# The second norm's second half is queued earlier, and three gate forms start 32 bytes further on

## The chip, the core and the metric

The kernel runs on one core of a Trainium2 chip. It is one program with five engines that run side by side and wait for each other through semaphores: PE (TensorE, matmuls; its weight loads have a row of their own, PEld), DVE (VectorE), ACT (ScalarE), POOL (GpSimd) and SP, which only issues DMAs. The metric is the device time of one execution in microseconds (us). Smaller is better.

## The reference, cut to what matters

One decoder layer for 512 tokens of width 1024, in float32. Two token mixers are merged; what this change touches comes behind them:

```python
x = x + rms_norm(mixed @ w_out, norm_mix_post)                      # first norm
h = rms_norm(x, norm_ffn_pre)                                       # second norm
f = (silu(h @ w_ffn_gate) * (h @ w_ffn_up)) @ w_ffn_down            # 1024 -> 2816 -> 1024
x = x + rms_norm(f, norm_ffn_post)
```

`rms_norm(x, g)` is `x * rsqrt(mean(x*x) + eps) * g`, with the mean over the 1024 channels of a token.

## The kernel before, in words

**Layout.** Channels lie on the 128 partitions, tokens along the free axis. So `x1[k]`, k = 0 to 7, is 128 channels by 512 tokens, and a mean over channels is a sum over partitions and over k. `halves[e]` are tokens 0 to 255 (e = 0) and 256 to 511 (e = 1). A float32 product is done as three matmuls in a rounded format: every operand is split into a high part and a low part (the rest), and high by high, high by low and low by high are added up in PSUM. Making such a pair ("a form") costs a copy on ACT for the high part and a subtraction on DVE for the low part, or two ACT steps and a DMA from POOL's queue that adds the raw matrix onto its negated high part (`dma_split`, L1523).

**The residual and the second norm.** `resid(e)` (L1413) multiplies the first norm's scale in, adds x and makes the high and low parts `h2h`, `h2l` (per k: DVE L1424, L1425, ACT L1426, DVE L1427). `resid_squares(e)` (L1431) squares `x1[k]` on ACT (L1436) and adds the eight squares up on POOL (L1439). `norm2_sums(e)` (L1443) sums them over the partitions with PE matmuls against ones (L251), makes mean + eps on DVE (L259) and takes the power -0.5 on POOL (L260). `norm2_scale(e, after)` (L1448) spreads the result over the partitions with PE (L268), and ACT copies it into `rb_x` (L1450).

**The channel mixer's first product.** `w_gate` and `w_up` have 22 column blocks of 128. The first three (`NPLAIN`) are plain products that need no scale beforehand, since the scale can be multiplied in afterwards. They cover the time in which the norm is made: `ffn_half(e, w, ps, ks)` (L1452) does, per row k, six matmuls of 256 tokens for gate and up of a block. Its weights are w0 and w1; the third block's, w2, run through `prod` with 512 tokens a matmul. From block N0 = 3 on, gate and up together are a 2 x 2 block matrix that is multiplied by the normalised `h` with seven half-size products in place of eight (a11, s2, s3, s1, a12, a22, s4; the scheme of Strassen and Winograd). A block of this kind is a unit (`unit(n)`, L1647), a product in it is twelve matmuls (L1662), and DVE adds its results together (L1668), which also frees the PSUM bank for the next. The units need the sums of the activations as forms of their own (b11, t2, t3, t1, b21, t4, b22), made once: `normed(e)` (L1606) multiplies the scale in, eight DVE steps a half (L1608); `x_form` (L1611) splits (high L1616, low L1617); `x_forms()` (L1627) makes the rest behind the second half's normalisation. Each unit also needs forms of its weights: `prep_g` (L1533) for the gate, `prep_u` (L1539) for a part of up, `prep_st` (L1574) for the four sums.

**Places.** Gate forms lie in turn in `wbuf` and in `g3`. `wbuf` holds two pairs of 1024 + 1024 columns; a pair starts `SHIFT` = 16 columns (64 bytes) further on, and for block N0+3 `TURN` = 8 columns (32 bytes) beyond that. `uub` has two halves, handed out in turn by `uu_half()` (L1340).

**What sets the order.** Each engine has one queue in an order fixed when the program is built, by dependences, by priorities and by the edges that the code adds: inside `tc.issue_after(x)` an instruction is queued behind x on x's engine. `tc.high_priority()` (used for the mean and the power) puts its instructions ahead where the data allow. `queued[...]` keeps instructions to queue others behind.

The calls around the change: `resid(1)` (L1767), rows 5 to 7 of w0's first half, `resid_squares(1)` (L1769), w1's first half with `norm2_sums(0)` in its middle, w0's second half with `norm2_scale(0)` behind its row 1, `normed(0)` and the form b11 (L1782 and L1783), w1's second half with `norm2_sums(1)` behind row 5 (L1784 to L1786), the first wide product of w2 with `norm2_scale(1)` behind its third row, form b21, `normed(1)`, and `x_forms()`.

Of the kernel before, what the change touches and what calls it, by code (L numbers as in the profile page):

```python
# [11 lines left out]
AF = mybir.ActivationFunctionType  # L12
OP = mybir.AluOpType
# [5 lines left out]
KD = D // 128  # L19
# [14 lines left out]
SHIFT = 16  # L34
TURN = 8
# [98 lines left out]
def hybrid_block_kernel(ctx: ExitStack, tc: tile.TileContext, I, outT):  # L134
    nc = tc.nc
    act, dve, pool, pe = nc.scalar, nc.vector, nc.gpsimd, nc.tensor
# [29 lines left out]
    g_fpre, g_fpost = vecs[:, 16:24], vecs[:, 24:32]  # L166
# [5 lines left out]
    rb_x = base.tile([128, S], F32, name="rb_x")  # L172
# [25 lines left out]
    for key in with_gla + with_cmp + with_att + late:  # L198
        kind, n = key
# [19 lines left out]
    def prod(ps, w, xh, xl, k0, kn, ktot, t=ALL):  # L219

        wh, wl = w
        marks = []
        for kk in range(kn):
            k = k0 + kk
            c = slice(kk * 128, (kk + 1) * 128)
            pe.matmul(ps[:, t], wh[:, c], xh(k)[:, t], start=(k == 0), stop=False)  # L226
            pe.matmul(ps[:, t], wh[:, c], xl(k)[:, t], start=False, stop=False)  # L227
            marks.append(pe.matmul(ps[:, t], wl[:, c], xh(k)[:, t], start=False, stop=(k == ktot - 1)))  # L228
        return marks
# [32 lines left out]
    broadcast, queued = [], {}  # L262
# [13 lines left out]
    for k in range(KD):  # L276
# [3 lines left out]
        if k == 0:  # L280
            act.activation(out=warm, in_=mhalf[:, 0:1], func=AF.Exp)
        last = act.activation(out=hT[:, k, :], in_=X[:, k], func=AF.Copy, scale=g_pre[:, k:k + 1])
        dve.scalar_tensor_tensor(out=hTl[:, k, :], in0=X[:, k], scalar=g_pre[:, k:k + 1],
                                 in1=hT[:, k, :].bitcast(F32), op0=OP.mult, op1=OP.subtract)
# [48 lines left out]
    halves = (slice(0, S // 2), slice(S // 2, S))  # L333
# [205 lines left out]
    for c in range(4):  # L539
        w = tk.next(("tok", 0, c))  # L540
# [78 lines left out]
    for j in range(NP):  # L619
# [6 lines left out]
        after = queued["dve"]  # L626
# [713 lines left out]
    def uu_half():  # L1340
        uturn[0] += 1
        return uub[:, 0:1024] if uturn[0] % 2 else uub[:, 1024:2048]
# [6 lines left out]
    def w_slot(which, shift=SHIFT):  # L1349

        if which == "w":
            return regions.next(shift)
        if which == "c":
            t = hlc(F32R, "w_hl")
            return [t[:, c:c + 1024] for c in (SHIFT, 1024 + SHIFT)]
        if which == "u":
            return uu_half(), uu_half()
        if which in ("d0", "d1"):
            t = wpair(which)
            return t[:, 0:1024], t[:, 1024:2048]  # L1360
        return tuple(wtile(t) for t in {"g3": ("g3h", "g3l"), "rw": ("rw", "rw")}[which])
# [6 lines left out]
    h2h, h2l = quads("h2h", 4, F32R, "hh"), quads("h2l", 2, F32R, "hl")  # L1368
    h2l23 = hlc(F32R, "h2l23")[:, 0:2048].rearrange("p (b a t) -> p b a t", b=2, a=2)
    h2l += [h2l23[:, i] for i in range(2)]  # L1370
    x1 = [slot(k) for k in range(8)]
# [41 lines left out]
    def resid(e, after=None, ks=range(KD), mult_after=None):  # L1413

        t = halves[e]
        if e not in rb_of:
            rb_of[e] = over_partitions(rs1, "tp", blocks[e], after)
        rb = rb_of[e]
        for k in ks:
            i, j = k // 2, k % 2  # L1420
            y = x1[k][:, t]
            hi, lo = h2h[i][:, j, t], h2l[i][:, j, t]
            with tc.issue_after(mult_after.ins) if mult_after else nullcontext():
                dve.tensor_tensor(out=y, in0=y, in1=rb[:, t], op=OP.mult)  # L1424
            dve.tensor_tensor(out=y, in0=y, in1=xs[i][:, j, t], op=OP.add)  # L1425
            last = act.activation(out=hi, in_=y, func=AF.Copy, scale=g_fpre[:, k:k + 1])  # L1426
            end = dve.scalar_tensor_tensor(out=lo, in0=y, scalar=g_fpre[:, k:k + 1], in1=hi.bitcast(F32),  # L1427
                                           op0=OP.mult, op1=OP.subtract)
        return last, end

    def resid_squares(e, ks=range(KD), after=None, squared_after=None):  # L1431
        t = halves[e]
        for k in ks:
            sq = sq2[0][:, t] if k == 0 else sq2[1 + (k - 1) % 6 // 2][:, halves[(k - 1) % 2]]
            with tc.issue_after(squared_after.ins) if squared_after else nullcontext():
                act.activation(out=sq, in_=x1[k][:, t], func=AF.Square)  # L1436
            if k > 0:
                with tc.issue_after(after.ins) if after else nullcontext():
                    pool.tensor_tensor(out=sq2[0][:, t], in0=sq2[0][:, t], in1=sq, op=OP.add)  # L1439

    rs2 = ffn.tile([128, NT], F32, name="rs2")

    def norm2_sums(e):  # L1443
        r = slice(2 * e, 2 * e + 2)
        ps = token_sums([sq2[0]], "tp", blocks[e])
        return rsqrt_mean(rs2[:, r], ps[:, r], D, EPS)

    def norm2_scale(e, after):  # L1448
        ps = over_partitions(rs2, "tp", blocks[e], after)
        return act.copy(rb_x[:, halves[e]], ps[:, halves[e]])  # L1450

    def ffn_half(e, w, ps, ks=range(KD)):  # L1452

        t = halves[e]
        marks = []
        for k in ks:
            i, j = k // 2, k % 2
            c = slice(k * 128, (k + 1) * 128)
            for x in range(2):
                wh, wl = w[x]  # L1460
                o = ps[x][:, t]
                pe.matmul(o, wh[:, c], h2h[i][:, j, t], start=(k == 0), stop=False)
                pe.matmul(o, wh[:, c], h2l[i][:, j, t], start=False, stop=False)
                last = pe.matmul(o, wl[:, c], h2h[i][:, j, t], start=False, stop=(k == KD - 1))
            marks.append(last)
        return marks
# [34 lines left out]
    N0 = NPLAIN  # L1501
# [29 lines left out]
        return minus  # L1531

    def prep_g(n, after=None):  # L1533
        hi, lo = w_slot(("w", "g3", "w")[(n - N0) % 3], SHIFT + (TURN if n == N0 + 3 else 0))
        minus = dma_split(n, hi, lo, raws[n, "w_gate"], I["w_gate"][n], after)
        forms[n, "a11"], forms[n, "a12"] = [(hi[:, c], lo[:, c]) for c in (slice(0, 512), slice(512, 1024))]
        return minus

    def prep_u(n, after=None, t=None):  # L1539
        t = uu_half() if t is None else t  # L1540
        hi, lo = t[:, 0:512], t[:, 512:1024]
        dma_split(n, hi, lo, ups[n][:, 512:1024], I["w_up"][n, :, 512:1024], after)
        forms[n, "a22"] = (hi, lo)
# [59 lines left out]

    XF = {}

    def normed(e):  # L1606
        for k in range(KD):
            dve.scalar_tensor_tensor(out=nb[k // 4][e][:, k % 4, :], in0=x1[k][:, halves[e]], scalar=g_fpre[:, k:k + 1],  # L1608
                                     in1=rb_x[:, halves[e]], op0=OP.mult, op1=OP.mult)

    def x_form(name, segs, after=None):  # L1611

# [144 lines left out]
    for n in (6, 7):  # L1757
        out_half(n, 1)
    sq2 = [t[:, i, :] for t in quads("sq2_", 2, F32, "e") for i in range(2)]
# [4 lines left out]
    on_act, on_dve = resid(0, None, range(KD - 1, KD), queued["mean"])  # L1764
    resid_squares(0, range(3, KD), root)
    marks = ffn_half(0, w0, first, range(3, 5))
    high_end, _ = resid(1, marks[-1])  # L1767
    ffn_half(0, w0, first, range(5, 8))
    resid_squares(1, range(KD), None, high_end)  # L1769
    split_pair(N0, s12, ("s1", "s2"), on_act, True)  # L1770
    w1 = (st.next(("g", 1)), st.next(("u", 1)))
    second = (bank("mm"), bank("mm"))
# [3 lines left out]
    marks = ffn_half(1, w0, first, range(0, 2))  # L1776
# [2 lines left out]
    nb = [[ffn.tile([128, 4, 256], F32, tag="a%d" % (2 * p + e), name="nb%d%d" % (p, e)) for e in range(2)]  # L1779
          for p in range(2)]  # L1780
    b11, b12, b21, b22 = [t.rearrange("p q t -> p (q t)") for t in (nb[0][0], nb[0][1], nb[1][0], nb[1][1])]
    normed(0)  # L1782
    x_form("b11", [(b11, *at(0))])  # L1783
    ffn_half(1, w1, second, range(0, 6))  # L1784
    scale_made = norm2_sums(1)
    ffn_half(1, w1, second, range(6, 8))  # L1786
    third = (bank("acc"), bank("acc"))

    def h2(p):
        return lambda k: p[k // 2][:, k % 2, :]  # L1790

    w2 = st.next(("g", 2))
    marks = prod(third[0], w2, h2(h2h), h2(h2l), 0, 3, KD)
    rb_made = norm2_scale(1, marks[-1])
    x_form("b21", [(b21, flat(quad("e0", F32R, "x4h")), flat(quad("e1", F32R, "x4l")))])
    normed(1)
    prod(third[0], [x[:, 384:1024] for x in w2], h2(h2h), h2(h2l), 3, 5, KD)
# [19 lines left out]
    for n in range(N0, KF):  # L1817
        if n + 2 < KF:
            load(n + 2, "w_gate")
            load(n + 2, "w_up")  # L1820
        last = unit(n, rest_of_forms if n == N0 else None,
                    (lambda copied: prep_u(N0 + 2, copied, uu_next)) if n == N0 + 2 else None)
        if n == N0:
            end = last
        if n == N0 + 1:
            plain_end()
            plain_out(2, *third)()
        if n + 1 < KF:
            prep_st(n + 1, end, plain_outs if n == N0 else None)
        if n + 2 < KF:  # L1830
            prep_g(n + 2, {N0 + 1: queued.get("s1cast"), N0 + 2: queued.get(("s34", N0 + 2)),
                           N0 + 3: queued.get(("s12", N0 + 4))}.get(n))
            if n == N0 + 1:
                uu_next = uu_half()
            if n > N0:
                prep_u(n + 2, queued["s1cast"] if n == N0 + 1 else None)
        if 2 * KH <= n < 2 * KH + 4:
            down_t3(n - 2 * KH)
# [352 lines left out]
```

## Time and profile before

| | us |
|---|---|
| median of 3 runs | 823.38 (822.57 to 823.55) |
| the profiled execution | 822.37 |
| its span, first to last instruction | 820.6 |
| PE busy | 813.5 |
| DVE busy | 649.5 |
| ACT busy | 523.6 |
| POOL busy | 177.4 |

The granted clock of TensorE was 1.00 of full speed (2.4 GHz) in the stretches around the change. A row of the order of time reads: start (us from the span's start), busy time, engine, line, operation, what it writes `<-` what it reads, the shape, the number of instructions merged into the row, and in brackets the idle time before it with what ended it. The busy time of one matmul row includes its way through the array, so the step from one start to the next, not the busy time, says how fast matmuls follow each other. A row of the waits reads: who `<-` for whom, total us, times, longest. A row of the stretches reads: window, its length, then busy time and number of instructions for PE, PEld, DVE, ACT and POOL, then the granted clock, the DMA engines' share and GB/s. Tiles go by the program's names without their numbers: `w_d`, `w_hl`, `w_g3h`, `w_rw`, `uub` and `wbuf` hold forms of weights, `hT_hi`, `hT_lo`, `x4h`, `x5h` and `x` forms of activations, `ps_...` are PSUM banks, `nb` the normalised activations, `sq` squares, `rs` the mean and its power.

### The profile page before, as it was taken

The page shows a single profiled execution, that of the slowest core. Times are in us where ns is not written, and L with a number is a line of the kernel's source. Part 1 is how long each engine was busy: PE and PEld are TensorE (multiplying, and loading weights), DVE is VectorE, ACT ScalarE, POOL GpSimd, SP SyncE. Part 2 cuts the span into 40 slices and gives each one's busy share as a digit, 9 for nine tenths or more (in the row PEclk, how much of TensorE's full clock was granted, in tenths as well). Part 3 has the DMA queues.
Part 4 walks back from the last instruction along what each step waited for, and adds up shares of the span by engine and source line. Part 5 has one row for each costly group of instructions (what it writes and reads, how often), then busy time and mean ns, then how long its engine had stood idle before and what let it go on. Part 6 is the DMA issues. An engine that isn't in the chain of part 4 may idle for free.

```text
span 820.6 us, 14977 instructions
## 1 busy us (share of the span) xinstructions
PE 813.5 (99%) x5676; PEld 750.2 (91%) x5676; DVE 649.5 (79%) x1219; ACT 523.6 (64%) x954; POOL 177.4 (22%) x221
## 2 busy tenths in 40 slices
PE   9999999999999999999999999999999999999997
PEld 8999999988888888888888999999999999889996
DVE  7878889955678988877675387997888778939885
ACT  7666697646536778887545577677655667536453
POOL 0242222312311111111001355012211110001264
PEclk9999999999999999999999999999999999999999
DMA  7588888411233354444238759589788882335323
GB/s 259 139 219 205 183 182 191 103 52 51 92 125 98 96 116 119 111 105 103 55 110 303 227 125 259 102 229 224 185 192 193 199 196 67 101 92 181 91 103 103
DMA packets 45449, 120.75 MB, mean 147 GB/s; under 512 B 5981, under 2 KB 11373, under 8 KB 45249
## 3 DMA queue, kind: packets, MB, share of 16 engines
q1 hardware_dynamic: 30576, 82.40, 30.1%
q0 software_dynamic: 14080, 36.76, 25.4%
q8 instruction: 44, 0.72, 0.3%
q10 hardware_dynamic: 720, 0.64, 0.2%
q14 instruction: 29, 0.23, 0.1%
HBM read 105.10 MB, written 4.19 MB: 133 GB/s over the span
## 4 chain that ended last, share of the span: by engine, by line
PE 93%; DVE 3%; ACT 2%; issue 1%; DMA 0%; SPq 0%; DVEq 0%; ACTq 0%
PE ps_sc L1662 7%; PE ps_mm L226 7%; PE ps_mm L227 6%; PE ps_mm L228 6%; PE ps_acc L1662 5%; PE ps_mm L1662 4%; PE ps_mm L446 4%; PE ps_tp L446 4%; PE ps_tp L1662 4%; PE ps_sc L1993 4%; PE ps_sc L446 3%; PE ps_acc L446 3%; PE ps_tp L1172 2%; PE ps_mm L1993 2%; PE ps_sc L227 1%; PE ps_sc L228 1%
## 5 line engine op out<-in xcount | busy, mean ns | idle before, releaser
L99 ACT CAST wbuf<-wraw 128x1024 fp32r<-128x1024 f32 (+3 forms) x56 | 54.1, 967 | 45.2 <-issue 11.1
L226 PE MATMUL ps_mm<-hT_hi,wbuf 128*128 128x512 f32 x152 | 61.8, 407 | 0.0
L106 DVE TENSOR_TENSOR wbuf<-wraw,wbuf 128x1024 fp32r<-128x1024 f32 (+3 forms) x41 | 44.3, 1082 | 20.6 <-ACT wbuf L99 16.3
L227 PE MATMUL ps_mm<-hT_lo,wbuf 128*128 128x512 f32 x152 | 60.0, 394 | 0.0
L228 PE MATMUL ps_mm<-hT_hi,wbuf 128*128 128x512 f32 x152 | 59.8, 394 | 0.0
L1548 ACT CAST w_d<-s 128x1024 fp32r<-128x1024 f32 x25 | 26.1, 1045 | 30.3 <-PE ps_acc L1662 13.9
L1131 ACT ACTIVATE p<-p,mx 128x512 f32<-128x512 f32 (+1 forms) x64 | 35.8, 560 | 9.2 <-DVE mx L1129 8.4
L244 DVE TENSOR_TENSOR pl<-ps_tp,ph 128x512 fp32r<-128x512 f32 (+1 forms) x64 | 31.2, 490 | 9.7 <-ACT ph L243 8.8
L1129 DVE CUSTOM_DVE_ANT_0 p<-ps_sc,causal 128x512 f32<-128x512 f32 (+1 forms) x64 | 30.0, 485 | 7.4 <-PE ps_sc L1122 7.2
L228 PEld LDWEIGHTS ps_mm<-hT_hi,wbuf 128*128 128x128 f32 x152 | 28.5, 188 | 6.5 <-DVE wbuf L106 0.4
L226 PEld LDWEIGHTS ps_mm<-hT_hi,wbuf 128*128 128x128 f32 x152 | 28.6, 188 | 5.5
L103 POOL DMA_DIRECT2D wbuf<-wraw x15 | 13.1, 875 | 94.3 <-ACT wbuf L102 94.3
L227 PEld LDWEIGHTS ps_mm<-hT_lo,wbuf 128*128 128x128 f32 x152 | 28.7, 189 | 4.5
L1530 POOL DMA_DIRECT2D wbuf<-in_w_gate x13 | 11.1, 856 | 89.1 <-ACT wbuf L1528 71.8
L243 ACT CAST ph<-ps_tp 128x512 fp32r<-128x512 f32 (+1 forms) x64 | 26.4, 414 | 6.1 <-PE ps_tp L1172 5.3
L1555 DVE TENSOR_TENSOR w_d<-s,w_d 128x1024 fp32r<-128x1024 f32 x24 | 29.3, 1220 | 0.0
L1172 PE MATMUL ps_tp<-ident,p 128*128 128x128 f32 x160 | 27.7, 272 | 0.0
L1172 PEld LDWEIGHTS ps_tp<-ident,p 128*128 128x128 f32 x160 | 20.8, 140 | 7.1
L226 PE MATMUL ps_mm<-gla_hi,wbuf 128*128 128x512 f32 x64 | 26.1, 407 | 0.0
L227 PE MATMUL ps_mm<-gla_lo,wbuf 128*128 128x512 f32 x64 | 25.2, 393 | 0.0
L228 PE MATMUL ps_mm<-gla_hi,wbuf 128*128 128x512 f32 x64 | 25.1, 393 | 0.0
L1548 ACT CAST w_hl<-s 128x1024 fp32r<-128x1024 f32 x11 | 11.5, 1046 | 18.2 <-PE ps_acc L1662 7.0
(981 smaller groups left out, 3210.5 us busy)
## 6 DMA issues: line engine op xcount, KB each, us to landing
wraw<-in_w_t SPq DMA_DIRECT2D x28, 512.0 KB, 3.6
wraw<-in_w_gate SPq DMA_DIRECT2D x21, 512.0 KB, 5.6
rw<-in_w_up SPq DMA_DIRECT2D x19, 512.0 KB, 6.7
wbuf<-wraw POOLq DMA_DIRECT2D x15, 512.0 KB, 4.5
wbuf<-in_w_gate POOLq DMA_DIRECT2D x13, 512.0 KB, 5.5
urw<-in_w_t SPq DMA_DIRECT2D x12, 512.0 KB, 5.5
uub<-in_w_up POOLq DMA_DIRECT2D x19, 256.0 KB, 7.3
raw<-in_w_down SPq DMA_DIRECT2D x10, 448.0 KB, 3.3
```

What stands on the lines that cost most here:

```text
L99: self.cast = self.nc.scalar.copy(hi[:, :cols], raw[:, :cols])
L106: self.nc.vector.tensor_tensor(out=lo[:, :cols], in0=raw[:, :cols], in1=hi[:, :cols].bitcast(F32), op=OP.subtract)
L226: pe.matmul(ps[:, t], wh[:, c], xh(k)[:, t], start=(k == 0), stop=False)
L227: pe.matmul(ps[:, t], wh[:, c], xl(k)[:, t], start=False, stop=False)
L228: marks.append(pe.matmul(ps[:, t], wl[:, c], xh(k)[:, t], start=False, stop=(k == ktot - 1)))
L244: return dve.tensor_tensor(out=lo, in0=src, in1=hi.bitcast(F32), op=OP.subtract)
L446: pe.matmul(o, w[:, c], x_of(b, q, low), start=(first and q == 0 and i == 0), stop=(q == 3 and i == 2), skip_group_check=True)
L1131: act.activation(out=o, in_=o, func=AF.Exp, scale=-1.0, bias=mx[:, i:i + 1], accum_out=z[:, i:i + 1])
L1172: queued["turn"] = pe.transpose(tp[:, i * 128:(i + 1) * 128], p[:, OFF[i] + k * 128:OFF[i] + (k + 1) * 128], ident)
L1548: cast = act.copy(hi, t)
L1662: last = pe.matmul(o, w[:, c], x[q], start=(first and q == 0 and i == 0), stop=(q == 3 and i == 2), skip_group_check=True)
L1993: pe.matmul(o, c, x[q], start=(first and n == 0 and i == 0), stop=(n == KH - 1 and i == 2), skip_group_check=True)
```

## The change

1. `second_squares` takes the place of `resid_squares(1)`. The first four squares are queued on ACT behind the high part of k = 5, the other four behind that of k = 7. POOL adds only the squares of k = 1 to 3; DVE adds those of 5 to 7 onto that of 4, behind the residual's last low part, and then the two sums.
2. Two of `normed(0)`'s eight steps are queued on DVE behind that last add, then the mean of the second half, then the other six. PE's sums for the second half move from behind row 5 of w1's second half to behind row 0, and the broadcast from behind the third row of w2 to behind row 4 of w1's second half: four rows behind the sums.
3. The gate forms of N0 and N0+2 start `TURN` further on, like that of N0+3.
4. `prep_u(N0 + 2)` is called in unit N0+1, behind the copy of its first product, not in unit N0+2; the half of `uub` is taken at the call.

```diff
@@ resid
-            last = act.activation(out=hi, in_=y, func=AF.Copy, scale=g_fpre[:, k:k + 1])
+            last = queued["high", e, k] = act.activation(out=hi, in_=y, func=AF.Copy, scale=g_fpre[:, k:k + 1])
@@ new
+    def second_squares(low_end):
+        t = halves[1]
+        sq = [sq2[0][:, t]] + [sq2[1 + (k - 1) % 6 // 2][:, halves[(k - 1) % 2]] for k in range(1, KD)]
+        for k in range(KD):
+            with tc.issue_after(queued["high", 1, 5 if k < 4 else 7].ins):
+                act.activation(out=sq[k], in_=x1[k][:, t], func=AF.Square)
+            if 0 < k < 4:
+                pool.tensor_tensor(out=sq[0], in0=sq[0], in1=sq[k], op=OP.add)
+            elif k > 4:
+                with tc.issue_after(low_end.ins):
+                    low_end = dve.tensor_tensor(out=sq[4], in0=sq[4], in1=sq[k], op=OP.add)
+        with tc.issue_after(low_end.ins):
+            queued["squares"] = dve.tensor_tensor(out=sq[0], in0=sq[0], in1=sq[4], op=OP.add)
@@ prep_g, prep_u
-        hi, lo = w_slot(("w", "g3", "w")[(n - N0) % 3], SHIFT + (TURN if n == N0 + 3 else 0))
+        hi, lo = w_slot(("w", "g3", "w")[(n - N0) % 3], SHIFT + (TURN if n - N0 in (0, 2, 3) else 0))
-    def prep_u(n, after=None, t=None):
-        t = uu_half() if t is None else t
+    def prep_u(n, after=None):
+        t = uu_half()
@@ normed
-    def normed(e):
-        for k in range(KD):
-            dve.scalar_tensor_tensor(...)
+    def normed(e, after=None, ks=range(KD)):
+        for k in ks:
+            with tc.issue_after(after.ins) if after else nullcontext():
+                dve.scalar_tensor_tensor(...)
@@ the calls
-    high_end, _ = resid(1, marks[-1])
+    _, low_end = resid(1, marks[-1])
     ffn_half(0, w0, first, range(5, 8))
-    resid_squares(1, range(KD), None, high_end)
+    second_squares(low_end)
...
-    normed(0)
+    normed(0, queued["squares"], range(0, 2))
+    ffn_half(1, w1, second, range(0, 1))
+    scale_made = norm2_sums(1)
+    normed(0, queued["mean"], range(2, KD))
     x_form("b11", [(b11, *at(0))])
-    ffn_half(1, w1, second, range(0, 6))
-    scale_made = norm2_sums(1)
-    ffn_half(1, w1, second, range(6, 8))
+    marks = ffn_half(1, w1, second, range(1, 5))
+    rb_made = norm2_scale(1, marks[-1])
+    ffn_half(1, w1, second, range(5, 8))
...
-    marks = prod(third[0], w2, h2(h2h), h2(h2l), 0, 3, KD)
-    rb_made = norm2_scale(1, marks[-1])
+    prod(third[0], w2, h2(h2h), h2(h2l), 0, 3, KD)
...
-                    (lambda copied: prep_u(N0 + 2, copied, uu_next)) if n == N0 + 2 else None)
+                    (lambda copied: prep_u(N0 + 2, copied)) if n == N0 + 1 else None)
...
-            if n == N0 + 1:
-                uu_next = uu_half()
```

More of the change, by code (lines that the diff above doesn't have):

```diff
@@ L1604, in hybrid_block_kernel @@
     XF = {}
-    def normed(e):
-        for k in range(KD):
-            dve.scalar_tensor_tensor(out=nb[k // 4][e][:, k % 4, :], in0=x1[k][:, halves[e]], scalar=g_fpre[:, k:k + 1],
-                                     in1=rb_x[:, halves[e]], op0=OP.mult, op1=OP.mult)
+    def normed(e, after=None, ks=range(KD)):
+        for k in ks:
+            with tc.issue_after(after.ins) if after else nullcontext():
+                dve.scalar_tensor_tensor(out=nb[k // 4][e][:, k % 4, :], in0=x1[k][:, halves[e]], scalar=g_fpre[:, k:k + 1],
+                                         in1=rb_x[:, halves[e]], op0=OP.mult, op1=OP.mult)
     def x_form(name, segs, after=None):
```

## The prediction

> **What bounds the kernel now.** I read the page first, for the engine that carries the chain of waits, and the busy time by stretches second.
>
> ```profile
> span 820.6 us, 14977 instructions
> PE 813.5 (99%) x5676; PEld 750.2 (91%) x5676; DVE 649.5 (79%) x1219; ACT 523.6 (64%) x954; POOL 177.4 (22%) x221
> ```
>
> ```profile
> core 0: us, PE busy (x) PEld busy (x) DVE busy (x) ACT busy (x) POOL busy (x), PEclk, DMA share, GB/s
> 514.71:554.83 40.12, 39.48 (x338) 39.15 (x337) 39.87 (x68) 27.10 (x43) 4.89 (x6) 1.00 0.68 167
> 554.83:592.91 38.08, 38.08 (x339) 38.08 (x338) 30.08 (x54) 24.89 (x38) 7.14 (x10) 1.00 0.88 211
> ```
>
> PE is busy for 99% of the span, so only two things can be gained: gaps in its stream, and matmuls that follow each other too slowly. The two stretches hold the same work, 28 half-size products each (units N0 to N0+3, then the next four). The first takes 2.04 us longer, and it is the one in which DVE has no room left (39.87 of 40.12 us busy). This 2.04 us is the ceiling of what an earlier second norm can return there. Next, the waits of 488 to 556 us and the order of time on DVE.
>
> ```profile
> DVE nb L1608 <- ACT rb_x L1450: 3.6, 2, 2.2
> PE ps_sc L1662 <- DVE us L1668: 0.6, 1, 0.6
> ```
>
> ```profile
> 493.83 0.88 DVE L1427 SCALAR_TENSOR_TENSOR h2l<-slot,vecs,h2h 128x256 fp32r<-128x256 f32 x2 [0.24 <-ACT h2h L1426]
> 496.95 5.32 DVE L1608 SCALAR_TENSOR_TENSOR nb<-slot,vecs,rb_x 128x256 f32<-128x256 f32 x8 [2.23 <-ACT rb_x L1450]
> 502.19 1.21 DVE L1617 TENSOR_TENSOR hT_lo<-nb,hT_hi 128x1024 fp32r<-128x1024 f32 x1
> 503.33 0.14 DVE L259 TENSOR_SCALAR rs<-ps_tp 128x2 f32<-128x2 f32 x1
> ...
> 506.35 3.26 DVE L1608 SCALAR_TENSOR_TENSOR nb<-slot,vecs,rb_x 128x256 f32<-128x256 f32 x8 [1.39 <-ACT rb_x L1450]
> ...
> 515.26 1.22 DVE L1617 TENSOR_TENSOR hT_lo<-t,hT_hi 128x1024 fp32r<-128x1024 f32 x1
> ...
> 530.78 0.41 DVE L1668 TENSOR_TENSOR us<-ps_sc,us 128x256 f32<-128x256 f32 x1
> ```
>
> From 506.35 DVE works off one queue without a pause; its start is set by the broadcast of the second half's scale. The low of t2 ends at 516.48 and PE wants it at that moment; an `add` that frees a bank is done only at 531.19, and PE stands.
>
> ```profile
> 488.40 0.36 PE L1462 MATMUL ps_mm<-h2h,w_g3h 128*128 128x256 f32 x1
> ...
> 491.31 0.28 PE L1462 MATMUL ps_sc<-h2h,wbuf 128*128 128x256 f32 x1
> ...
> 497.26 0.28 PE L1462 MATMUL ps_mm<-h2h,w_g3h 128*128 128x256 f32 x1
> ...
> 501.34 0.50 PE L251 MATMUL ps_tp<-consts,sq 128*128 128x1 f32 x4
> 501.70 0.36 PE L1462 MATMUL ps_mm<-h2h,w_g3h 128*128 128x256 f32 x1
> ...
> 505.29 0.61 PE L268 MATMUL ps_tp<-ident,rs 128*128 128x128 f32 x4
> ...
> 514.71 0.28 PE L1662 MATMUL ps_tp<-hT_hi,wbuf 128*128 128x256 f32 x1
> ...
> 516.12 0.28 PE L1662 MATMUL ps_tp<-hT_hi,w_d 128*128 128x256 f32 x1
> ...
> 516.48 0.36 PE L1662 MATMUL ps_sc<-hT_hi,w_g3l 128*128 128x256 f32 x1
> 516.67 0.28 PE L1662 MATMUL ps_tp<-hT_lo,w_d 128*128 128x256 f32 x1
> ...
> 531.25 0.39 PE L1662 MATMUL ps_sc<-hT_hi,w_hl 128*128 128x256 f32 x1 [0.64 <-DVE us L1668]
> ...
> 550.66 0.28 PE L1662 MATMUL ps_mm<-x4h,wbuf 128*128 128x256 f32 x1
> ...
> 552.10 0.28 PE L1662 MATMUL ps_acc<-x5h,uub 128*128 128x256 f32 x1
> 553.47 1.52 PE L1662 MATMUL ps_acc<-x,w_d 128*128 128x256 f32 x12
> 554.83 0.28 PE L1662 MATMUL ps_tp<-hT_hi,w_g3h 128*128 128x256 f32 x1
> ```
>
> A product of twelve matmuls takes 1.36 us at its best (553.47 to 554.83), 1.41 in unit N0's first (514.71 to 516.12), and 1.44 with the gate form that is already shifted by 32 bytes (550.66 to 552.10).
>
> **The change, part by part.** *Squares.* ACT, POOL and DVE now:
>
> ```profile
> 490.44 1.29 ACT L1426 ACTIVATE h2h<-slot,vecs 128x256 fp32r<-128x256 f32 x3
> ...
> 494.11 2.55 ACT L1436 ACTIVATE sq<-slot 128x256 f32<-128x256 f32 x8
> ...
> 505.94 0.37 ACT L1450 COPY rb_x<-ps_tp 128x256 f32<-128x256 f32 x1 [1.71 <-PE ps_tp L268]
> ```
>
> ```profile
> 494.90 1.56 POOL L1439 TENSOR_TENSOR sq<-sq 128x256 f32<-128x256 f32 x2 [2.54 <-ACT sq L1436]
> 496.54 3.38 POOL L1439 TENSOR_TENSOR sq<-sq,sq 128x256 f32<-128x256 f32 x4
> 499.99 0.80 POOL L1439 TENSOR_TENSOR sq<-sq 128x256 f32<-128x256 f32 x1
> 503.55 0.71 POOL L260 TENSOR_TENSOR rs<-rs,consts 128x2 f32<-128x2 f32 x1 [2.75 <-DVE rs L259]
> ```
>
> One square is 0.32 us (2.55 by 8). Four move behind the high of k=5, done at 491.73, where ACT has 1.5 us of room (to 494.11, less two highs of 0.43) for 1.3. The other four end near 495.5. POOL keeps three adds, about 2.4 us from 492.4. They run beside the residual's last DVE steps, and that costs: eight normalisations took 5.32 us beside about five POOL adds and 3.26 without, 0.4 us an add, so the residual's end moves from 494.71 to 495.9 at most. The last of PE's rows that read them begins at 496.6 (0.68 before 497.26), so I cost that at nothing; with that cover gone it would be at most the same 1.2 us. DVE's four new adds, 0.41 each, end between 496.4 (not held up) and 497.5 (held up). The old chain ended on POOL at 500.79.
>
> *Sums.* They now stand behind row 0 of w1's second half, which begins at 497.26 and lasts 0.68 (half of 1.36): 497.94. So the squares lead by 0.4 to 1.5 us. I take no wait; the bound of one is in the rivals.
>
> *Mean.* On DVE it stands behind two normalisations, and waits for the sums. Queued behind it are six normalisations. The two end between 497.2 and 498.3, the sums at 498.30 (0.36 us), the mean at about 498.6: DVE loses up to 1.2 us. PE does not wait for that. POOL's power takes 0.71: about 499.4.
>
> *Broadcast.* Four rows behind the sums. The 24 matmuls that follow the first half's sums took 2.91 us (488.40 to 491.31): 501.21, so the scale leads by 1.8 us. From the broadcast's start to the end of ACT's copy it took 1.02 (505.29 to 506.31): 502.2, which is 4.1 us sooner than now. These 24 are above the best 2.72 by 0.19, but now two rows and nine wide matmuls lie there, so I count PE's time up to 514.71 as unchanged (between -0.1 and +0.1).
>
> *DVE's queue.* Six normalisations without POOL beside them (0.41 each) end at 501.1, the two lows of b11 and b21 at 1.2 each at 503.5, and the second half's normalisations begin there, not at 506.35. So DVE's queue for the units starts 2.85 us sooner, of the 4.1; the lows of the first half are late next. The t2 low is then done at 513.6, three us before PE's need; the `add` of 531.19 near 528.3.
>
> *Shift.* N0's and N0+2's gate forms join N0+3's. Four products go to 1.44: three from 1.36, one from 1.41: +0.08 x 3 + 0.03 = +0.27, about 0.3 with the first matmuls of the product behind each. No other work hides it, for PE is the chain. The other way, it could come back if N0's first product at 1.41 is the start of a slower stretch that the shifted form ends; that is within the 0.1 of this term.
> By the Trainium skill, "SBUF — State Buffer", section "Who interferes with whom", PE's two read ports are its own and it never waits on anyone, so a start address would cost nothing, and the sum would be 0.3 lower. The trace disagrees with that: 1.44 against 1.36 for the same twelve matmuls.
>
> *The up form of N0+2* (two ACT steps, one DMA on POOL's queue) is issued one unit sooner, behind the copy of N0+1's first product.
>
> ```profile
> 520.60 0.37 ACT L1681 COPY us<-ps_sc 128x256 f32<-128x256 f32 x1 [1.45 <-PE ps_sc L1662]
> 524.58 0.63 ACT L1590 CAST w_hl<-s 128x512 fp32r<-128x512 f32 x1 [3.61 <-DVE s L1565]
> ```
>
> ACT idles 3.61 us there, so it costs nothing; were the half of `uub` still being read, what is behind it (the cast of N0+1's sums) could slip by at most these two steps, some 1.2 us. On POOL its DMA passes no step of the norm: the last of those, at 503.55, is long over.
>
> *Sum.* Of the 2.04 us, two products at 1.44 (0.16) and one at 1.41 (0.05) are pace; 1.83 is waiting in many small pieces, from 0.08 (516.48 to 516.67, against 0.11) to about 0.8 (the 0.64 and the refilling around it). With all waits gone the gain is 1.83 - 0.3 = 1.5. But DVE still does 1.2 us steps in front of `add`s that free a bank, and PE's order is fixed at build, so I leave 0.3 for three or four small waits: 1.2 us. The profiled execution took 822.37 (span 820.6 and 1.8 around it), so 821.2. The median of the runs is 1.0 above it: 823.38 - 1.2 = 822.2. That is 0.15%; about 0.2%, or 1.65 us, is what a measurement can tell from no change.
>
> **The rivals.** *All waits go, and more* (chance 0.22): no wait is left in the units (1.5), PE's time up to 514.71 falls by its 0.1, and N0's shifted first product ends a slower stretch (0.1): 1.7, 821.7, or up to 0.3 below that if both ends of the small terms add up. For it: the lead of three us. Against: DVE stays the fullest helper.
>
> *The shift is free* (0.04): all six shifted products run at 1.36, as twelve matmuls can. Then the 0.3 is not paid and N0+3's 0.16 comes back: 1.2 + 0.3 + 0.16 = 1.7, 821.7. Against it: the 1.44. That is what the rule of the Trainium skill's page "SBUF — State Buffer" above would give.
>
> *The queue refills* (0.20): the lead is used up by DVE standing at the mean and by `add`s that are placed behind long steps, so the 0.64 wait or its like returns; or the order made at build does not place the sums where the text has them. Gain 0.8 to nothing, with the shift's 0.3 paid: 823.1.
>
> *PE waits at the sums* (0.08), the other side. POOL's adds and DVE's two-input steps hold each other up, and the last add ends as late as POOL's chain did, 500.79 + 0.41 = 501.2. PE then stands 3.3 us at 497.94, and the units still gain at most 1.5: 825.2. It decides from a last add after 499.4 (no gain) and 501.1 (slower by 1.65). Against: four adds fewer on POOL, and ACT's first squares 2.4 us sooner.
>
> **How the numbers follow.** Forecast 822.2, gain 0.8 to 1.6, chance 0.46. Faster by over 0.2%: the first two rivals, 0.26. Slower: 0.08. Within: 0.46 + 0.20 = 0.66. The range from 821.3 to 823.9 holds all but the last rival and some spread of the runs, which lie 1.0 apart.
>
> **What would show it.** Right: sums near 498, broadcast near 501.2, the second normalisations near 503.5, units N0 to N0+3 in 38.6 to 39.0 us, no PE wait over 0.3 there. Wrong: a PE wait in front of the sums; the first two shifted forms at 1.36; the four units at 39.8 or more; or twelve-matmul products behind 555 us off 1.36.

## The result and the profile after

The changed kernel takes 827.86 us (826.06 to 828.47, 5 runs), the kernel before, run beside it, 822.61 (822.49 to 823.55, 5 runs): a ratio of 1.0054, 95% interval 1.0043 to 1.0065. It is slower by 5.2 us, where 1.2 us of gain was forecast. The profiled execution took 828.23, its span is 826.4, 5.8 more than before.

The first lines of the page after, then the busy time by stretches for the two sets of four units (window, length, PE, PEld, DVE, ACT, POOL, granted clock, share of the DMA engines, GB/s):

```profile
span 826.4 us, 14975 instructions
PE 816.9 (99%) x5676; PEld 753.3 (91%) x5676; DVE 648.9 (79%) x1223; ACT 523.7 (63%) x954; POOL 176.1 (21%) x217
```

```profile
514.93:560.71 45.78, 42.61 (x337) 41.99 (x336) 40.19 (x67) 30.31 (x46) 5.18 (x7) 0.93 0.75 175
560.71:598.79 38.08, 38.08 (x338) 38.08 (x337) 29.66 (x54) 23.51 (x37) 6.80 (x9) 1.00 0.80 196
```

Unit N0 begins at 514.93 (before 514.71), and the four units behind N0+3 take their 38.08 as before. So the loss lies whole in N0 to N0+3: 45.78 us in place of 40.12, 5.66 more, with the clock at 0.93 on average.

What was moved came out on time. DVE's, PE's and ACT's order of time after the change:

```profile
497.28 0.42 DVE L1453 TENSOR_TENSOR sq<-sq,sq 128x256 f32<-128x256 f32 x1
497.62 0.88 DVE L1623 SCALAR_TENSOR_TENSOR nb<-slot,vecs,rb_x 128x256 f32<-128x256 f32 x2
498.65 0.16 DVE L259 TENSOR_SCALAR rs<-ps_tp 128x2 f32<-128x2 f32 x1 [0.15 <-PE ps_tp L251]
...
503.52 3.25 DVE L1623 SCALAR_TENSOR_TENSOR nb<-slot,vecs,rb_x 128x256 f32<-128x256 f32 x8
...
516.33 1.22 DVE L1632 TENSOR_TENSOR hT_lo<-t,hT_hi 128x1024 fp32r<-128x1024 f32 x1 [3.82 <-ACT hT_hi L1631]
```

```profile
498.12 0.50 PE L251 MATMUL ps_tp<-consts,sq 128*128 128x1 f32 x4
501.38 0.61 PE L268 MATMUL ps_tp<-ident,rs 128*128 128x128 f32 x4
```

```profile
502.25 0.36 ACT L1464 COPY rb_x<-ps_tp 128x256 f32<-128x256 f32 x1
502.51 1.05 ACT L1540 CAST wbuf<-wraw 128x1024 fp32r<-128x1024 f32 x1
508.89 0.62 ACT L1540 CAST uub<-rw 128x512 fp32r<-128x512 f32 x1 [5.32 <-DMA rw<-in_w_up]
...
513.43 1.28 ACT L1504 ACT_TABLE_LOAD   x1
514.72 0.63 ACT L1504 ACTIVATE fa<-fa 128x512 f32<-128x512 f32 x1
515.26 1.04 ACT L1631 CAST hT_hi<-t 128x1024 fp32r<-128x1024 f32 x1
...
520.08 1.04 ACT L1631 CAST x5h<-nb 128x1024 fp32r<-128x1024 f32 x1
521.02 0.36 ACT L1696 COPY us<-ps_tp 128x256 f32<-128x256 f32 x1
```

The last lines are where it goes wrong. At 503.56 ACT comes to the cast of N0+1's up form (`uub<-rw`, L1540), whose raw block has not landed, and stands 5.32 us. Behind it in ACT's queue is everything that the units wait for: N0+1's gate form, a silu, the high part of t2 (515.26; before 513.00), and, behind five more highs of activations and one of weights, the copy of N0's first product, which frees a PSUM bank (521.02; before 516.78). DVE, which had t2 ready at 509.64, idles 3.82 us for t2's high. PE's waits:

```profile
PE ps_tp L1677 <- ACT us L1696: 2.3, 1, 2.3
PE ps_tp L1677 <- DVE hT_lo L1632: 0.9, 1, 0.9
```

Two things made that stand. ACT's order is new: before, N0+1's gate form went first and gave the block 1.9 us more. And the block itself came later. From issue to landing (the last figure, us), before and after:

```profile
rw<-in_w_up SPq DMA_DIRECT2D x1, 512.0 KB, 4.0
```

```profile
wbuf<-in_w_gate POOLq DMA_DIRECT2D x1, 512.0 KB, 8.7
rw<-in_w_up SPq DMA_DIRECT2D x1, 512.0 KB, 8.1
```

Before, it was issued at 502.27 and landed at 506.31; after, it was issued at 500.74 and landed at 508.81. The load that shares its time is POOL's, which adds N0's raw gate onto its form. That one is queued behind the second half's scale (`scale_made`), and the scale is now 4.7 us sooner. POOL's order of time before, and after:

```profile
504.79 0.92 POOL L1530 DMA_DIRECT2D wbuf<-in_w_gate  x1 [0.53 <-ACT uub L1528]
```

```profile
498.89 0.89 POOL L260 TENSOR_TENSOR rs<-rs,consts 128x2 f32<-128x2 f32 x1 [3.79 <-DVE rs L259]
500.23 0.92 POOL L1544 DMA_DIRECT2D wbuf<-in_w_gate  x1 [0.45 <-issue]
```

With PE's two waits the granted clock fell as well, to 0.50 (1.2 GHz) from 520.4, within the second wait, to 527.2. By stretches, and three of PE's rows:

```profile
520.00:522.00 2.00, 0.56 (x2) 0.56 (x3) 1.81 (x2) 1.39 (x3) 0.00 (x0) 0.59 1.13 224
522.00:524.00 2.00, 2.00 (x12) 2.00 (x11) 1.91 (x4) 0.00 (x0) 0.00 (x0) 0.50 0.37 70
...
526.00:528.00 2.00, 2.00 (x14) 2.00 (x13) 1.19 (x4) 0.62 (x1) 0.00 (x0) 0.70 0.00 0
```

```profile
522.03 0.63 PE L1677 MATMUL ps_tp<-hT_hi,w_d 128*128 128x256 f32 x2
522.46 0.41 PE L1677 MATMUL ps_tp<-hT_lo,w_d 128*128 128x256 f32 x1
522.67 0.63 PE L1677 MATMUL ps_tp<-hT_hi,w_d 128*128 128x256 f32 x2
```

PE is busy throughout from 522, and yet three matmuls take 0.64 us there (522.03 to 522.67): they start 213 ns apart, against 113 at full clock. There are 25 such steps, from 521.82 to 527.15, which is 2.5 us more than at 113 ns. (The counts in the rows by stretches hold matmuls that straddle a bound in both stretches, so they do not serve for this.) So the 5.66 us are: waits 3.2 in place of 0.6 (+2.6), the lower clock +2.5, and about 0.5 of smaller terms. Among these are short stops around the waits and a slower pace behind them (matmuls 118 ns apart in place of 113, to 541); some short stops of the kernel before are gone.

In some executions everything behind the first 26 us of the program lies 2 to 2.6 us later (the kernel before seems to have it too: of 35 runs of it 8 took 824.51 us or more, the others 823.52 or less), so the length of the four units is the better measure of an effect of that size.

### The profile page after: what moved, and what is told of

It reads as the page before. It is cut to its first block, busy times and chain, and to the rows that moved or that the text cites. A ratio compares the mean times of both kernels' runs of the same rounds, so it can differ in the third digit from the quotient of the medians.

```text
span 826.4 us, 14975 instructions
## 1 busy us (share of the span) xinstructions
PE 816.9 (99%) x5676; PEld 753.3 (91%) x5676; DVE 648.9 (79%) x1223; ACT 523.7 (63%) x954; POOL 176.1 (21%) x217
## 4 chain that ended last, share of the span: by engine, by line
PE 92%; DMA 2%; DVE 2%; ACT 2%; issue 1%; POOL 0%; SPq 0%; ACTq 0%; DVEq 0%; POOLq 0%
PE ps_sc L1677 7%; PE ps_mm L226 6%; PE ps_mm L227 6%; PE ps_mm L228 6%; PE ps_acc L1677 5%; PE ps_tp L1677 5%; PE ps_mm L1677 4%; PE ps_mm L446 4%; PE ps_tp L446 4%; PE ps_sc L2008 4%; PE ps_sc L446 3%; PE ps_acc L446 3%; PE ps_tp L1172 2%; PE ps_mm L2008 2%; PE ps_sc L228 1%; PE ps_sc L226 1%
## 5 line engine op out<-in xcount | busy, mean ns | idle before, releaser
L1544 POOL DMA_DIRECT2D uub<-in_w_up x19 | 16.6, 875 | 31.6 <-ACT uub L1542 29.1
```

## The experiments

The theory to test is that **ACT's queue stands on a late transfer**. It needs the new order on ACT and the late landing. Rivals: the shift costs more than thought; PE lost the matmuls of N0+1 that it used to slip into N0's waits.

**The up form of N0+1 behind its gate form.**

```diff
-    prep_g(N0 + 1)
-    prep_u(N0 + 1)
+    prep_u(N0 + 1, prep_g(N0 + 1))
```

> The changed kernel with one edge more on ACT: the two steps of N0+1's up form stand behind those of its gate form, as in the kernel before. Theory (ACT's queue stands for 5.3 us at the cast of N0+1's raw up block, whose DMA lands at 508.8, and all highs behind it come late): ACT reaches that cast near 506.8 and stands for about 2 us; the high of t2 ends near 513.7 and not 516.3, PE's 0.9 us wait goes and the 2.3 us wait for the copy of N0's first product falls to some 0.4; no low clock; 822.0 us (821.3 to 823.0). Rival A (the shift by 32 bytes costs the time): no change, 827 to 828. Rival B (PE has lost the products of N0+1 that it did in between before): PE still stands at s2 and s3, 825 or more.

822.95 us beside 823.19, ratio 0.9995 (0.9978 to 1.0012). The units, PE's wait in them and ACT's at the cast:

```profile
517.17:557.07 39.90, 39.59 (x337) 39.03 (x336) 37.70 (x66) 26.60 (x42) 5.18 (x7) 1.00 0.73 174
```

```profile
PE ps_sc L1677 <- DVE us L1683: 0.3, 1, 0.3
ACT uub L1540 <- DMA rw<-in_w_up: 1.7, 1, 1.7
```

One edge on ACT takes 5.88 of the units' 45.78 us away, and the low clock with them. The shift and the scale's new place are still in it, so neither is the cost by itself. Nor are the lost fill-ins: N0's products follow each other here, as in the changed kernel, with no matmul of N0+1 between them.

**The copy of N0's first product ahead of two highs.** The highs of t4 and b22 are queued behind that copy instead of behind t3's.

```diff
-    ..., flat(quad("e3", F32R, "x5l")))], hi_made)
+    ..., flat(quad("e3", F32R, "x5l")))], copied)
```

> The changed kernel with another edge on ACT alone: the highs of t4 and b22 stand behind the copy of N0's first product, as in the kernel before. Theory: the stand of 5.3 us at the up cast stays, so t2's high still ends at 516.3 and the 0.9 us wait stays; the copy goes near 519.1 and not 521.0, so the 2.3 us wait falls to about 0.4; 824 to 826 us. Rival A: no change, 827 to 828. Rival B: no change.

826.5 us, ratio 1.0038 (1.0022 to 1.0054).

```profile
517.30:560.41 43.11, 40.56 (x338) 39.44 (x336) 39.58 (x67) 30.88 (x47) 5.70 (x8) 1.00 0.81 184
```

```profile
ACT uub L1540 <- DMA rw<-in_w_up: 5.9, 1, 5.9
PE ps_tp L1677 <- DVE us L1683: 1.0, 1, 1.0
PE ps_tp L1677 <- DVE hT_lo L1632: 0.9, 1, 0.9
```

The wait of 2.3 us for the copy goes, and the clock stays at 1.00, but ACT's stand stays and PE waits in smaller pieces for DVE, which is late for the same reason. It mends a consequence, and 2.7 us of the units' length come back. The time is half a us above the range expected, for I had not seen the wait of 1.0 us.

**Both.** The two edits together.

```diff
-    prep_g(N0 + 1)
-    prep_u(N0 + 1)
+    prep_u(N0 + 1, prep_g(N0 + 1))
...
-    ..., flat(quad("e3", F32R, "x5l")))], hi_made)
+    ..., flat(quad("e3", F32R, "x5l")))], copied)
```

> Both edges together (up form behind gate form; highs of t4 and b22 behind the copy). Theory: no PE wait over 0.3 us in units N0 to N0+3, these four in 38.6 to 39.2 us; 821.5 us (821.0 to 822.3), a little below the kernel before. Rival A: 827 to 828. Rival B: above 824.

822.25 us beside 823.19, ratio 0.9989 (0.9976 to 1.0002). The units take 39.55, and PE has no wait in them that the profile lists:

```profile
514.85:554.40 39.55, 39.55 (x338) 39.22 (x336) 37.91 (x66) 27.26 (x43) 5.18 (x7) 1.00 0.71 170
```

So most of the units' loss is undone by the first edge alone, and by the units' length the two together gain 0.57 us over the kernel before; the times cannot tell that from no change. The units stay 0.35 us above the 39.2 that I had put as the upper end.

**The early scale without the shift, and with the up form of N0+2 where it was.**

```diff
-        hi, lo = w_slot(..., SHIFT + (TURN if n - N0 in (0, 2, 3) else 0))
+        hi, lo = w_slot(..., SHIFT + (TURN if n == N0 + 3 else 0))
...
-                    (lambda copied: prep_u(N0 + 2, copied)) if n == N0 + 1 else None)
+                    (lambda copied: prep_u(N0 + 2, copied, uu_next)) if n == N0 + 2 else None)
```

> The changed kernel without the shift of N0's and N0+2's forms and with the up form of N0+2 made in unit N0+2 as before: the earlier norm alone. Theory: ACT has the same order up to unit N0, so it stands for the same 5 us at the up cast, PE waits about 3 us in N0 and the clock falls; 827 to 829 us, more than the changed kernel if the slow steps of 118 ns are ended only by N0+3's form. Rival A (the shift): 822 to 823. Rival B: 827 to 828.

832.26 us, ratio 1.0097 (1.0074 to 1.012): slower still.

```profile
516.83:565.05 48.22, 42.89 (x337) 42.06 (x336) 40.46 (x67) 30.33 (x46) 5.19 (x7) 0.93 0.73 164
```

```profile
PE ps_tp L1677 <- ACT us L1696: 2.3, 1, 2.3
PE ps_sc L1677 <- DMA uub<-in_w_up: 2.2, 1, 2.2
PE ps_tp L1677 <- DVE hT_lo L1632: 0.7, 1, 0.7
```

The two waits of the changed kernel are there without the shift, which ends that rival. The third I had not expected, and with it the time lies above my range: left at its old place, N0+2's up form lands 2.2 us after PE wants it. ACT's queue is late in this run as well (it stands 5.1 us), so whether the old place would cost that with ACT's orders mended is not tested. The clock fell twice here, the second time behind that one wait of 2.2 us (0.50 from 551.8 to 555.2).

**POOL's load of N0's gate put off.** A copy of one column on POOL reads the raw up block of N0+1, and the load is queued behind it; ACT's order stays as the change made it.

```diff
+    landed = pool.tensor_copy(out=..., in_=raws[N0 + 1, "w_up"][:, 0:1])
+    with tc.issue_after(landed.ins):
+        pool.dma_start(lo, src, accum_op=OP.add)      # N0's gate form
```

> The changed kernel, with one thing put off: POOL's accumulating DMA of N0's gate form waits until the raw up block of N0+1 has landed (a 128x1 copy on POOL reads that block first). ACT's order is left as the change made it, with N0+1's up cast ahead of its gate form. Theory (two transfers that used to follow each other now share the DMA engines, and ACT's queue stands on the one that it needs): the up block lands 4 to 5 us after its issue instead of 8.1, at about 505; ACT's stand at the cast falls from 5.32 to 1 to 2 us, PE's waits in the units from 3.2 to under 1 us, and the time to 822 to 825. Rival (the block is late because of the stores of x1 that run at the same time, or for a reason of its own queue): it still takes about 8 us, ACT stands 5 us, and the time stays at 826 to 828.5. A cost that either could meet: N0's gate form now lands near 513 instead of 509, and PE reads its low half at about 515.

823.85 us beside 822.93, ratio 1.0009 (1.0000 to 1.0019). The units, the landing of the block, then ACT's wait for it and PE's:

```profile
516.92:557.69 40.77, 40.13 (x337) 39.27 (x336) 38.57 (x66) 27.50 (x43) 5.18 (x7) 1.00 0.85 197
```

```profile
rw<-in_w_up SPq DMA_DIRECT2D x1, 512.0 KB, 5.7
```

```profile
ACT uub L1540 <- DMA rw<-in_w_up: 2.7, 1, 2.7
PE ps_tp L1680 <- ACT us L1699: 0.6, 1, 0.6
```

With the other load out of the way the block takes 5.7 us in place of 8.1, the stand halves and 5.0 us of the units' length come back. So the collision is shown, and it is the larger part of the delay. It is not all: 5.7 is not 4.0, and the stand is 2.7 where I had expected 1 to 2. Until 505.68 the stores of `x1` still run here, 3.2 us beside the block; before, they overlapped it by 1.4. The load of N0+1's gate, issued just ahead of it on the same queue, also runs longer beside it: 4.4 us here (to 506.89), 2.7 before (to 504.92). Which of the two makes the rest no run separates. The Trainium skill, "DMA: Bandwidth & Descriptors", section "Issuing engines are not separate DMA queues", says that DMAs issued by different engines run on the same 16 engines and interleave; the 8.1 and 5.7 us agree.

**The shift alone, on the kernel before.**

```diff
-        hi, lo = w_slot(..., SHIFT + (TURN if n == N0 + 3 else 0))
+        hi, lo = w_slot(..., SHIFT + (TURN if n - N0 in (0, 2, 3) else 0))
```

> The kernel before, with nothing but the gate forms of N0 and N0+2 shifted by 32 bytes. Theory (the time went at ACT's queue, not into the shift): four products go from 1.36 or 1.41 to 1.44 us, so between 0.1 and 0.4 us slower, less whatever step of 118 ns a shifted form ends in the products behind it: 822.8 to 823.6 beside 823.2, units N0 to N0+3 in 39.9 to 40.5. Rival (the shift is what cost the time): 825.5 to 828, units in 43 to 46.

822.96 beside 822.93, ratio 0.9998 (0.9987 to 1.0008); units in 40.20, against 40.12. It costs next to nothing by itself.

```profile
515.02:555.22 40.20, 39.64 (x338) 39.39 (x336) 39.92 (x68) 27.10 (x43) 4.90 (x6) 1.00 0.69 169
```

**The new order on ACT alone, on the kernel before.** N0+1's gate form behind its up form.

```diff
-    prep_g(N0 + 1)
-    prep_u(N0 + 1)
+    prep_g(N0 + 1, prep_u(N0 + 1))
```

> The kernel before, with one order changed: on ACT the up form of N0+1 goes ahead of its gate form, as it came to stand in the changed kernel. Everything else, the time of the second half's scale and of the transfers above all, stays as before. Theory (the stand needs both, the early order and a block that lands late): the raw up block still lands about 506.3, ACT comes to it at about 506.2, so the stand is under 0.5 us and the time within 0.5 us of the kernel before: 822.5 to 823.5. Rival (the order alone is the cost): ACT stands 2 us or more there and the time is 825 or more.

824.96 beside 824.75, ratio 1.0014 (0.9992 to 1.0037). ACT has no wait at that cast, for the block takes its old time; instead the gate form, now second, is 0.5 us late for PE:

```profile
rw<-in_w_up SPq DMA_DIRECT2D x1, 512.0 KB, 4.1
```

```profile
PE ps_sc L1663 <- DVE us L1669: 0.5, 1, 0.5
PE ps_sc L1663 <- DMA w_g3l<-in_w_gate: 0.5, 1, 0.5
```

The order alone does not make the stand. It takes the late block as well, as the theory has it.

**Both orders mended, and no shift.** On the kernel with both edges:

```diff
-        hi, lo = w_slot(..., SHIFT + (TURN if n - N0 in (0, 2, 3) else 0))
+        hi, lo = w_slot(..., SHIFT + (TURN if n == N0 + 3 else 0))
```

> The changed kernel with both orders on ACT mended (the up form of N0+1 behind its gate form; the highs of t4 and b22 behind the copy of N0's first product) and without the shift of N0 and N0+2. It is the mended kernel of 822.25 but for the shift, with PE never waiting in the units. Theory (a matmul step of 118 ns, once entered, stays until something like a shifted form ends it): the products from N0 to N0+2 keep 1.41 us, units in 39.6 to 40.2 instead of 39.55, time 822.3 to 823.0. Rival (the shift only costs): its four products at 1.36 instead of 1.44, units in 39.2, time 821.9.

822.68 beside 822.93, ratio 0.9992 (0.9981 to 1.0003).

```profile
516.71:556.01 39.30, 39.30 (x337) 38.79 (x336) 37.28 (x65) 26.47 (x42) 5.18 (x7) 1.00 0.69 171
```

39.30 against 39.55 with the shift: by the units my theory missed and its rival was right. The slower steps of 118 ns do not stay until a shifted form ends them; without the shift there are fewer of them (45 of 336 steps are of 116 to 119 ns, with it 101).

**The up form of N0+1 behind t1's high**, with the copy ahead of two highs, and with the shift.

```diff
-        x_form("t1", [(b11, *at(3))], hi_made)
+        queued["t1"] = x_form("t1", [(b11, *at(3))], hi_made)[0]
...
-    prep_u(N0 + 1)
+    prep_u(N0 + 1, queued["t1"])
```

> The changed kernel with the highs of t4 and b22 behind the copy of N0's first product, and with the up form of N0+1 put on ACT behind t1's high, so that ACT stands on no transfer between the broadcast and the units. Theory (with ACT's two orders mended no wait of PE is left in the units, so nothing further is gained by a shorter stand): ACT's stand of 2.2 us goes, t2's high comes 1 to 2 us sooner, and the time stays within 0.4 us of the 822.25 of the kernel with both orders mended: 821.9 to 822.6. Rival (the up form, 6 us later, lands after its product wants it, as N0+2's did without its earlier place): a wait of 1 to 2 us at the product of N0+1's up form, time 823.5 to 825.

822.45 beside 822.93, ratio 0.9990 (0.9980 to 1.0000). ACT waits for no load here, t2's high starts at 509.71, and the units take what they took with both edges, within 0.1:

```profile
514.98:554.46 39.48, 39.48 (x338) 39.25 (x336) 37.13 (x65) 26.19 (x41) 6.05 (x8) 1.00 0.71 172
```

So the 2.2 us that ACT still stood with both edges were covered.

**The same without the shift.** On the kernel of the experiment just told:

```diff
-        hi, lo = w_slot(..., SHIFT + (TURN if n - N0 in (0, 2, 3) else 0))
+        hi, lo = w_slot(..., SHIFT + (TURN if n == N0 + 3 else 0))
```

> The changed kernel with the up form of N0+1 behind t1's high, the highs of t4 and b22 behind the copy of N0's first product, and no shift of N0 and N0+2. Theory (PE waits for nothing in the units and the shift costs 0.08 us at each of its products, with some products behind it at 118 ns): units in 39.1 to 39.4 beside 39.48 with the shift, time 0.1 to 0.4 us below the 822.45 of that one: 822.0 to 822.4. Rival (the shift spares a collision that comes back without it): units in 39.5 to 40.2, time 822.5 to 823.2.

821.88 us beside 824.75, ratio 0.9972 (0.9962 to 0.9983): it is the shortest of all, and beats both kernels.

```profile
514.91:554.15 39.24, 39.24 (x337) 38.78 (x336) 37.16 (x65) 26.01 (x41) 6.06 (x8) 1.00 0.72 172
```

Of the 2.87 us between the medians only 0.88 is the units' (39.24 against 40.12), and the lowest runs of the two kernels lie 0.90 apart as well (821.64 and 822.54). By both of these it gains 0.9 us. Without the shift the units are 0.24 us shorter than with it.

**The changed kernel again**, unedited, for the clock's share.

> The changed kernel as it is, to size what the lower clock adds to the waits: one of its five runs so far kept the granted clock at 1.00 and took 826.06, four had a mean of 0.994 or 0.995 and took 827.8 to 828.5. Theory (the two gaps of 0.9 and 2.3 us cost 3.2 and the clock that falls behind them 2 to 3.5 more, in the runs in which it falls): runs with a mean of 1.00 at 825.5 to 826.5, those with 0.994 to 0.995 at 827.5 to 828.5. Rival (the clock has little to do with the time): no such order among the runs.

828.82 beside 824.75, ratio 1.0053 (1.0032 to 1.0074). ACT stood 5.7 us and PE's two waits came back at 2.3 and 0.9. The clock:

```profile
522.00:524.00 2.00, 2.00 (x15) 2.00 (x16) 2.00 (x4) 0.00 (x0) 0.00 (x0) 0.88 0.62 121
524.00:526.00 2.00, 2.00 (x11) 2.00 (x11) 1.97 (x4) 0.00 (x0) 0.00 (x0) 0.50 0.00 0
526.00:528.00 2.00, 2.00 (x16) 2.00 (x15) 1.86 (x5) 1.26 (x3) 0.00 (x0) 0.76 0.00 0
```

Here the low clock began 1.5 us after PE had gone on, and lasted from 523.5 to 527.0. By the starts of the matmuls, 15 steps are of 213 ns and two more are lengthened: 1.6 us, against 2.5 in the first profile. The runs did not sort by their mean clock as I had expected: the one with 1.00 took 828.74, in the middle of the six. So the clock's part is read from the trace of each execution, 1.6 and 2.5 us in these two, not from the times.

## Why the prediction was wrong, point by point

- *Squares, sums, mean, broadcast*: right. The last add ended at 497.70 (forecast 496.4 to 497.5), the sums began at 498.12 without a wait (497.94), the mean at 498.65 (498.6), the broadcast at 501.38 (501.21), the copy ended at 502.61 (502.2). The rival "PE waits at the sums" did not come.
- *DVE's queue*, the step that failed. Its first half held: the second half's normalisations began at 503.52 (forecast 503.5). Its second half did not: "the t2 low is then done at 513.6" counted DVE's steps alone. That low needs ACT's high of the same form, and ACT had stood 5.3 us; the low started at 516.33 and was done at 517.55, four us later than forecast. The sum had no term for a stand of ACT: 3.2 us of it came through to PE as waits, and the lower clock took 2.5 more.
- What was missing before that step: I moved the scale and counted what it gives to DVE, and not what else was queued on it. Two edges hang on it: POOL's load of N0's gate form (`scale_made`) and ACT's forms of N0+1 (`rb_made`). The first came 4.6 us sooner, into the time of the up block's load; the second moved as well, and ACT's forms of N0+1 came out in a new order, the up form first; that the one made the other is not shown. ACT was read as an engine with room (27.10 of 40.12 us busy), which says nothing of what stands at the head of its queue.
- *Shift*: about right, in part by luck. Forecast 0.3; 0.25 and 0.24 in the two pairs with and without it where PE has no wait, 0.08 on the kernel before. In those pairs 36 or 37 more steps of 120 ns cost the 0.24 of the forecast, more steps of 118 ns cost 0.2 to 0.3 besides, and fewer single long steps gave as much back. The Trainium skill, "SBUF — State Buffer", section "Who interferes with whom", says that PE has two read ports of its own and never waits on another engine; it says nothing of start addresses, so that a shift would then be free was my own step, and the pairs do not bear it out.
- *The up form of N0+2* at its new place: right that it costs nothing, for no wait of PE on it is listed. In the one run with it at the old place PE waited 2.2 us for it, which I had not seen.
- *Sum*: 1.2 with the shift. With the orders mended it is 0.57 and 0.64, and without the shift 0.82 and 0.88. No wait of PE is listed there, so the 1.83 put down to waiting was too high. Of the 2.04 us, 0.81 was the one stop at 530.33 (a step of 0.92 us), and that is about what comes back. Another 0.78 were ten single steps of 0.15 to 0.23 us, and these do not go with the waits: seven such steps, 0.76 us, are left in the shortest run. What they wait for the profile does not list. With the shift, the slower steps of 118 ns (101 and 119 of 336, against 41 before) take about 0.3 more.
- *The rivals*: "The queue refills" named the right kind of thing, the order made at build, and put it at DVE, with the loss of the gain as the worst. The chance for slower, 0.08, sat on the sums alone. A fall of the clock behind a wait was in no case.

What stays open: why the builder put the up form first (its ready times are not in a trace), and how the part of the late landing that POOL's load does not explain divides between the stores and the load of N0+1's gate.

## What to carry to other kernels

When a step is moved forward, list every instruction that waits for it or is queued behind it, on all engines, the DMAs first, and ask what each will now run beside. Then lay out again the queue of every engine that gets work from it: a strict queue with one cast at its head that waits for a load holds back everything behind it, however idle the engine is by its busy share. And keep loads that are wanted soon ahead of loads that are not, for a release that comes sooner can make them share.

## What the runs showed of the hardware that was not expected

- The granted clock of PE fell to 0.50 (1.2 GHz) at two waits of 0.9 and 2.3 us with 1.3 us of work between them: in the first profile within the second wait, in the second 1.5 us after it. It stayed there although PE was busy again, for 5.7 us of work in the first and 3.4 us in the second. It cost 2.5 and 1.6 us beside the 3.2 us of the waits. In the run without the shift it also fell behind a single wait of 2.2 us. With waits of 0.9 and 1.0 us (the second experiment) the stretch kept 1.00.
- Matmuls of one kind follow each other 113, 118 or 120 ns apart at a granted clock of 1.00. Where a shifted form is read, ten steps of 120 follow each other; single ones also stand among the steps of 118. 118 comes in stretches: after the low clock it held from 528 to 541, and with both edges, where N0+2's shifted form is read between other products, from 527.8 to 536.5. What starts and ends it is open; leaving the shift out took more than half of it away.
- A 512 KB load took 4.0, 5.7 or 8.1 us by what ran beside it.
